# A hybrid mixer and MoE block on one core: whole-block transfers for all ten places of the weights' ring

## The chip, the cores and the metric

The kernel runs on one core of a Trainium2 chip. The metric is the device time of one execution in microseconds (us); lower is better. Three runs of the kernel before give a median of 1217.1 us (1215.6 to 1217.73).

## The reference, cut to what matters

One transformer block over 256 tokens of width 1024, all in float32:

```python
mod = jax.nn.silu(c) @ w_ada[l] + b_ada[l]                  # six rows: sh1, sc1, ga1, sh2, sc2, ga2
h = rms_norm(x, norm_w[l, 0]) * (1 + sc1) + sh1
y = hybrid_mixer(h, w_in[l], conv_w[l], a_log[l], dt_bias[l], a_norm_w[l], rel_bias[l], w_out[l])
x = x + ga1 * rms_norm(y, norm_w[l, 1])
h = rms_norm(x, norm_w[l, 2]) * (1 + sc2) + sh2
y = moe_ffn(h, w_router[l], b_router[l], w_up[l], b_up[l], w_down[l], b_down[l])
x = x + ga2 * rms_norm(y, norm_w[l, 3])
```

`hybrid_mixer` is a gated delta rule (4 heads of 128, chunks of 64 tokens) beside an attention over a band of chunks with a relative bias (8 heads of 64). `moe_ffn` routes each token to 4 of 32 experts:

```python
hu = xe @ w_up[e] + b_up[e]
glu = jnp.minimum(hu[:, :D_EXPERT], 7.0)
lin = jnp.clip(hu[:, D_EXPERT:], -7.0, 7.0)
act = glu * jax.nn.sigmoid(1.702 * glu) * (lin + 1)
out = act @ w_down[e] + b_down[e]
```

`w_up[e]` is 1024 x 2048 and `w_down[e]` 1024 x 1024, so one expert has 12.6 MB of weights and the 32 experts 402.7 MB; each is read once.

## The kernel before, in words

The mixer comes first, then the router, then the experts. The weights of the mixer are packed on the host into blocks of 2 MB, 128 partitions by 4096 floats (`wpre`); `wload` (L79) brings one block into one buffer in one transfer, `hload` (L84) in two halves. The weights of each expert are packed likewise as six blocks of 2 MB (`wexp`), here called chunks: chunks 0 to 3 are the four quarters of `w_up`, chunks 4 and 5 the halves of `w_down`.

**Groups.** The experts are worked off in 14 groups, written as `ORDER = "PQPPSQPPSQPPPP"`: P is a pair of experts with 64 token places each, Q four experts with 32, S a single one with 128. `group` (L1119) runs chunks 0 to 5 in order. For a chunk, `eload` (L1101) issues the loads of that chunk for every expert of the group, and `expert_mm` (L1112) multiplies: its outer loop runs over the eight slices k of the contraction and its inner loop over the experts, so that with P the two experts' matmuls alternate (L1117). Behind the chunks 0 and 1, and 2 and 3, comes the activation (`act`, on DVE and ACT) and four transposes of its result (L1145); chunks 4 and 5 read the transposed result, the first four slices from chunks 0 and 1, the last four from chunks 2 and 3. The result of a down chunk is copied (L1163) and spread to the tokens by four matmuls (L1166).

**The ring.** The loads go round a ring of ten places of 2 MB, `RINGTAGS` (L23): wB, w0, wC, wE, w1, wD, wF, wh, wA, wx. Both w0 and w1 are printed as `w_f` in the trace. Eight places are fixed blocks of 16 KB in each partition. The other two are each put together from two pool tiles of 8 KB: "wh" from two tiles of tag wh, "wx" from one tile of tag wh and one of tag h2. `wslot` (L1092) hands them out. A place of two tiles needs two transfers, and `eload` then splits every load of the same chunk in two:

```python
m = 8 // max(pieces, max(len(ts) for ts in tss))
```

The transfers are issued first halves first, one for each expert, then second halves. `PIECES = {0: 2, 1: 2, 2: 2}` (L34) asks for halves for chunk 5 of group 0 and for all chunks of groups 1 and 2; the last chunk of the last group goes in four pieces of 512 KB.

**Order.** All these loads are issued by SP, one queue in program order. From group 1 on the experts' numbers come from the routing (`sig`, cast by DVE at L1218), and SP reads each of them with a load of its own (L1276) before the group's first transfer. A scheduler orders the instructions of each engine when the kernel is built; the source gives it the order of emission, pools and dependencies.

**The mixer's buffers.** The pool tag wh (3 tiles) also holds the high halves that `split` (L205) makes of the mixer's float32 blocks; tag h2 holds in turn `xt`, `whx`, `strip` (the relative bias, loaded at L748, masked by POOL at L750, added to the scores by DVE at L767) and `yb`. `delta_out` (L882) transposes the delta rule's output, 128 tokens at a time (L893), and splits it into two halves (ACT L896, DVE L897); the output projection's matmuls (L231) read those.

**Down biases.** `b_down` is loaded in group 1 in two pieces of 64 KB (`bdn`), each just ahead of the two matmuls that use it (L1294).

Of the kernel before, what the change touches and what calls it, by code (L numbers as in the profile page):

```python
# [8 lines left out]
F32 = mybir.dt.float32  # L9
F32R = mybir.dt.float32r  # L10
# [10 lines left out]
D = 1024  # L21
NE = 32
RINGTAGS = ["wB", "w0", "wC", "wE", "w1", "wD", "wF", "wh", "wA", "wx"]  # L23
PB = {"mm": 3, "dl": 3, "tp": 2}
# [8 lines left out]
ZPOS = [0, 2, 0, 0]  # L33
PIECES = {0: 2, 1: 2, 2: 2}  # L34


SINGLES, QUADS = 2, 3
ORDER = "PQPPSQPPSQPPPP"
WH = 3
RS_N = -2.0 * (-2.0 * (-2.0) ** 3) ** 3  # L40
# [9 lines left out]
def block_kernel(ctx, tc, x, small, rows, rel_ext, wpre, wexp, b_up, b_down, out,  # L50
                 dbg=None, stop=None):
    nc = tc.nc
    P = 128
# [6 lines left out]


    base = (nc.sbuf_base + 31) // 32 * 32
    ctx.enter_context(nc.sbuf_tensor("fixed", [P, 8 * 4096], F32))
    fixed = {}
    for i, tag in enumerate(("w0", "w1", "wA", "wB", "wC", "wD", "wE", "wF")):
        fixed[tag] = [nc.alloc_sbuf_tensor_at(f"{tag}_{d_}", (P, 4096), dt, offset=base + 16384 * i).ap()
                      for d_, dt in (("f", F32), ("r", F32R))]
# [25 lines left out]
    def k2(name, shape=(P, 512), dt=F32):  # L93
        return mem.tile(list(shape), dt, tag="k2", bufs=K2, name=name)
# [76 lines left out]

    xt = mem.tile([P, 2, D], F32, tag="h2", name="xt")
    csil = const.tile([P, 8], F32, name="csil")
# [29 lines left out]
    nsp = [0]  # L203

    def split(w, kv=None, steps=1, extra=None, copy=None):  # L205


        sr, wl = w
        kv = kv or KV
        wh = extra  # L210
        if wh is None:
            wh = mem.tile([P, 2048], F32, tag="wh", bufs=WH, name="wh").bitcast(F32R)
        kn = sr.shape[1]
        wh = wh.rearrange("p (k n) -> p k n", k=kn)
# [125 lines left out]
    kqT = mem.tile([P, 4, 2, 256], F32, tag="acc", name="kqT")  # L340
    whx = mem.tile([P, 2048], F32R, tag="h2", name="whx")
    spr = bank("dl")
# [403 lines left out]
    def attention(blS):  # L746
        strip = mem.tile([P, 8, 256], F32, tag="h2", name="strip")
        nc.sync.dma_start(strip, bass.AP(tensor=rel_ext.tensor, offset=rel_ext.offset,  # L748
# [114 lines left out]
    pos = steps(mixed(), 17)  # L863
    yb = mem.tile([P, 2, D], F32, tag="h2", name="yb")
    wo.append(hload(19, "w1", 4))
# [226 lines left out]
    def wslot(tag):  # L1092

        if tag in ("wh", "wx"):
            ts = [mem.tile([P, 2048], F32, tag="wh", bufs=WH, name="wh") if tag == "wh" or i == 0 else
                  mem.tile([P, 2048], F32, tag="h2", name="wx") for i in range(2)]
        else:
            ts = [block(tag)]
        return [t.rearrange("p (k n) -> p k n", n=512) for t in ts]
# [19 lines left out]
    def group(load, xg, wt, sels, first=False, mid=None, done=None):  # L1119
# [155 lines left out]
    for gi, grp in enumerate(groups):  # L1275
# [7 lines left out]
        if gi + 1 < len(groups):  # L1283
            ohog = prep(groups[gi + 1])
        cur = group(lambda j: eload(regs, j, 4 if (gi, j) == (len(groups) - 1, 5) else PIECES.get(gi, 1) if gi or j == 5 else 1), cur[0], cur[1], sels, gi == 0, mid, done if gi == len(groups) - 1 else None)
        if gi == 1:
            overflow()

            for n in range(2):
                bdn = k2("bdn", (NE, 512))  # L1290
                nc.sync.dma_start(bdn, b_down[:, n * 512:(n + 1) * 512])
                for a in range(2):
                    b_ = bank("tp")
                    T.matmul(b_, tqs[:, 256 + a * 128:256 + (a + 1) * 128], bdn, start=True, stop=True)  # L1294
                    V.tensor_add(acc[:, a, n * 512:(n + 1) * 512], acc[:, a, n * 512:(n + 1) * 512], b_)
# [100 lines left out]
```

## Time and profile before

| | before |
|---|---|
| median of 3 runs | 1217.1 us (1215.6 to 1217.73) |
| the profiled execution | 1217.74 us, of which the span of the trace is 1215.9 us |
| PE busy | 1052.1 us (87%) |
| DVE, ACT, POOL busy | 371.0, 192.8, 93.8 us (31%, 16%, 8%) |
| mean granted clock of TensorE | 0.942 |
| moved by DMA | 451.95 MB, 372 GB/s over the span |

In the trace's rows PE is the matrix engine (PEld its weight loads), DVE, ACT and POOL the vector, scalar and general engines, SP the engine that issues the loads, and SPq its queue. A row of the timeline has start, duration (both us), engine, line, operation, output<-inputs, count, and in brackets the idle time just before and who ended it. A matmul of `expert_mm` appears as two rows. A row of the DMA view has the transfers of one kind: count, KB of one, and the median time in us from issue to landing. A window's row is explained at its first use.

### The profile page before, as it was taken

The numbers are of one execution on the slowest core, as the hardware profiler recorded it, in microseconds if no ns is written. First come the engines' busy times: TensorE is split into PE (matmuls) and PEld (weight loads), VectorE is DVE, ScalarE is ACT, GpSimd is POOL, SyncE is SP. The second block draws the span as 40 slices with busy tenths as digits, with TensorE's granted clock in tenths as the row PEclk, the third lists the DMA queues.
The fourth block names the chain that finished last, engine by engine and source line by source line (L and its number), as shares of the span: only waits on it lengthen the run. The fifth ranks groups of instructions, "written<-read, shape, count | busy, mean of one in ns | idle before, by whom it ended". The sixth has DMA issues, their size and how long they took to land. (4 is left out here: it accounts for less than half of the span.)

```text
span 1215.9 us, 14799 instructions
## 1 busy us (share of the span) xinstructions
PE 1052.1 (87%) x5891; PEld 502.7 (41%) x5891; DVE 371.0 (31%) x852; ACT 192.8 (16%) x392; POOL 93.8 (8%) x61
## 2 busy tenths in 40 slices
PE   4878999999987799999996779989976798898995
PEld 2667997683431133334431133434421142333331
DVE  5587888564202112121211002122211011111113
ACT  3544315331101001010100001010100001010101
POOL 1435424010000000000000000000000000000001
PEclk9989999979998899999997899999997799999998
DMA  9923455696999999999999999999999999999993
GB/s 362 390 76 139 143 208 241 263 424 221 420 421 420 421 416 410 430 422 424 428 415 426 424 423 429 424 427 425 419 427 424 423 427 422 427 424 423 428 419 130
DMA packets 51464, 451.95 MB, mean 372 GB/s; under 512 B 5760, under 2 KB 7424, under 8 KB 9408
## 3 DMA queue, kind: packets, MB, share of 16 engines
q1 hardware_dynamic: 51392, 450.97, 89.6%
q8 instruction: 48, 0.79, 0.3%
q14 instruction: 24, 0.20, 0.0%
HBM read 449.50 MB, written 1.05 MB: 371 GB/s over the span
## 5 line engine op out<-in xcount | busy, mean ns | idle before, releaser
L1117 PE MATMUL dl<-w_f,xg 128*64 128x512 f32 (+1 forms) x224 | 114.8, 659 | 10.9 <-DMA w_f<-in_wexp_dram 10.9
L1171 DVE TENSOR_TENSOR acc<-acc,mm 128x512 f32<-128x512 f32 x52 | 35.8, 688 | 240.8 <-PE mm L1166 240.8
L1117 PE MATMUL mm<-w_f,xg 128*64 128x512 f32 (+2 forms) x208 | 94.4, 603 | 4.8 <-DMA w_f<-in_wexp_dram 4.8
L1273 POOL TENSOR_TENSOR wF_f<-acc,m_row 128x512 f32<-128x512 f32 x3 | 3.8, 1275 | 948.0 <-DVE acc L1171 948.0
L1117 PE MATMUL dl<-wh,xg 128*64 128x512 f32 (+2 forms) x144 | 70.2, 631 | 3.9 <-DMA wh<-in_wexp_dram 3.9
L1117 PE MATMUL dl<-wD_f,xg 128*64 128x512 f32 (+1 forms) x128 | 65.3, 661 | 3.3 <-DMA wD_f<-in_wexp_dram 3.3
L1117 PE MATMUL dl<-wE_f,xg 128*64 128x512 f32 (+2 forms) x112 | 56.7, 660 | 9.5 <-DMA wE_f<-in_wexp_dram 9.5
L1166 PE MATMUL mm<-yg,wts 128*128 128x512 f32 x112 | 54.5, 614 | 11.7 <-ACT yg L1163 10.7
L1135 ACT ACTIVATE sg<-gm 128x512 f32<-128x512 f32 x28 | 17.7, 631 | 289.1 <-DVE gm L1133 265.2
L1117 PE MATMUL mm<-wB_f,xg 128*64 128x512 f32 (+2 forms) x128 | 59.3, 610 | 0.0
L1117 PE MATMUL dl<-wC_f,xg 128*64 128x512 f32 (+2 forms) x112 | 56.7, 652 | 2.5 <-DMA wC_f<-in_wexp_dram 2.5
L1117 PE MATMUL dl<-wF_f,xg 128*64 128x512 f32 (+2 forms) x112 | 54.8, 628 | 3.0 <-DMA wF_f<-in_wexp_dram 3.0
L1117 PE MATMUL mm<-wh,xg 128*64 128x512 f32 (+1 forms) x144 | 56.8, 594 | 0.0
L998 PEld LDWEIGHTS tp<-oh,x 128*128 128x128 f32 x432 | 50.8, 193 | 12.2 <-issue 10.4
L998 PE MATMUL tp<-oh,x 128*128 128x128 f32 x432 | 54.7, 280 | 0.7 <-ACT aT__3401 L1146 0.7
L1117 PE MATMUL mm<-wE_f,xg 128*64 128x512 f32 (+1 forms) x112 | 49.6, 594 | 2.9 <-DMA wE_f<-in_wexp_dram 2.9
L1117 PE MATMUL dl<-wB_f,xg 128*32 128x512 f32 (+1 forms) x96 | 49.0, 647 | 3.5 <-DMA wB_f<-in_wexp_dram 3.5
L1008 DVE TENSOR_SCALAR xg<-tp,mc,mc 128x128 f32<-128x128 f32 x52 | 19.6, 406 | 104.0 <-PE dl L1117 95.3
L1163 ACT COPY yg<-dl 128x512 f32<-128x512 f32 x27 | 15.8, 586 | 223.7 <-PE dl L1117 223.7
L1117 PE MATMUL mm<-wC_f,xg 128*64 128x512 f32 (+1 forms) x112 | 50.0, 594 | 0.0
L1133 DVE TENSOR_SCALAR gm<-dl 128x512 f32<-128x512 f32 x14 | 9.7, 692 | 128.7 <-PE dl L1128 128.7
L1117 PEld LDWEIGHTS dl<-w_f,xg 128*64 128x64 f32 (+1 forms) x224 | 28.2, 135 | 45.6 <-issue 25.5
(634 smaller groups left out, 2244.8 us busy)
## 6 DMA issues: line engine op xcount, KB each, us to landing
wh<-in_wexp_dram SPq DMA_DIRECT2D x57, 1024.0 KB, 24.6
w_f<-in_wexp_dram SPq DMA_DIRECT2D x26, 2048.0 KB, 25.8
wA_f<-in_wexp_dram SPq DMA_DIRECT2D x36, 1024.0 KB, 22.2
wF_f<-in_wexp_dram SPq DMA_DIRECT2D x36, 1024.0 KB, 29.5
wE_f<-in_wexp_dram SPq DMA_DIRECT2D x15, 2048.0 KB, 29.4
wC_f<-in_wexp_dram SPq DMA_DIRECT2D x15, 2048.0 KB, 27.0
wB_f<-in_wexp_dram SPq DMA_DIRECT2D x13, 2048.0 KB, 22.1
wD_f<-in_wexp_dram SPq DMA_DIRECT2D x13, 2048.0 KB, 34.2
```

The lines of the kernel that those rows point to most:

```text
L998: T.matmul(b_[:, k * 128:(k + 1) * 128], x2[:, a, half(n)][:, k * 128:(k + 1) * 128], oh[:, a], start=a == tiles[0], stop=a == tiles[-1])
L1008: V.tensor_scalar(xg[:, k], src, mc, sc, op0=ALU.mult, op1=ALU.add)
L1117: T.matmul(b_[i * n:(i + 1) * n, :], lhs[:, k, i * n:(i + 1) * n], w(k), start=k == 0, stop=last and k == 7)
L1133: V.tensor_scalar(gm, bs[0], 7.0, None, op0=ALU.min)
L1135: S.activation(sg, gm, AF.Sigmoid, scale=1.702)
L1163: S.copy(yg, b_)
L1166: T.matmul(cb, wt[:, a], yg, start=True, stop=True)
L1171: V.tensor_add(acc[:, a, sl], acc[:, a, sl], cb)
L1273: (V if a and n else G).tensor_mul(fin[:, 0, a, sl], acc[:, a, sl], m3_row[:, sl])
```

## The change

Two more fixed blocks, wG and wH, take the places of "wh" and "wx", so that all ten places are alike. `wslot` is gone; `eload` issues one transfer of 2 MB for each place, two for chunk 5 of group 0, and four for the last chunk of the last group. The lower half of wH and the two halves of wG hold the high halves that `split` makes, in turn; the upper half of wH (`h2`) holds what tag h2 held. In the first group the matmuls of chunks 0 and 1 are emitted under a manual schedule of PE. `b_down` is loaded as one tile ahead of the groups. The later lines shift by up to 5 up or down: L1109 becomes L1104, L1117 becomes L1112, L1276 becomes L1280, L893 becomes L898.

```diff
-RINGTAGS = ["wB", "w0", "wC", "wE", "w1", "wD", "wF", "wh", "wA", "wx"]
+RINGTAGS = ["wB", "w0", "wC", "wE", "w1", "wD", "wF", "wG", "wA", "wH"]
...
-PIECES = {0: 2, 1: 2, 2: 2}
...
-    ctx.enter_context(nc.sbuf_tensor("fixed", [P, 8 * 4096], F32))
+    ctx.enter_context(nc.sbuf_tensor("fixed", [P, 10 * 4096], F32))
...
+    highs = [fixed["wH"][1][:, 0:2048], fixed["wG"][1][:, 0:2048], fixed["wG"][1][:, 2048:4096]]
+
+    def h2(dt=0):
+        return fixed["wH"][dt][:, 2048:4096]
...
-    xt = mem.tile([P, 2, D], F32, tag="h2", name="xt")
+    xt = h2().rearrange("p (a n) -> p a n", a=2)
...
-            wh = mem.tile([P, 2048], F32, tag="wh", bufs=WH, name="wh").bitcast(F32R)
+            wh = highs[nsp[0] % 3]
+            nsp[0] += 1
...
-        strip = mem.tile([P, 8, 256], F32, tag="h2", name="strip")
+        strip = h2().rearrange("p (h k) -> p h k", h=8)
...
-        tss = [wslot(slot()) for _ in regs]
-        m = 8 // max(pieces, max(len(ts) for ts in tss))
+        ts = [block(slot()).rearrange("p (k n) -> p k n", n=512) for _ in regs]
+        m = 8 // pieces
...
-        b0 = up(0, load(0))
-        g0 = act([b0, up(1, load(1))])
+        if first:
+
+            with tc.manual_schedule(engines={mybir.EngineType.PE}):
+                b0 = up(0, load(0))
+                b0b = up(1, load(1))
+            g0 = act([b0, b0b])
+        else:
+            b0 = up(0, load(0))
+            g0 = act([b0, up(1, load(1))])
...
+    bdn = mem.tile([NE, D], F32, tag="ga2", name="bdn")
+    nc.sync.dma_start(bdn, b_down)
...
-        cur = group(lambda j: eload(regs, j, 4 if (gi, j) == (len(groups) - 1, 5) else PIECES.get(gi, 1) if gi or j == 5 else 1), cur[0], cur[1], sels, gi == 0, mid, done if gi == len(groups) - 1 else None)
+        cur = group(lambda j: eload(regs, j, 4 if (gi, j) == (len(groups) - 1, 5) else 2 if (gi, j) == (0, 5) else 1), cur[0], cur[1], sels, gi == 0, mid, done if gi == len(groups) - 1 else None)
```

The change also moves instructions. On PE, the rows of the first group's chunks 0 and 1 read the same before and after, names and lines apart: under the manual schedule some matmuls of chunks 2 and 3 (on wF and wh, now wG) still stand among those of chunk 0. At the end of the mixer the eight transposes of `delta_out`, of which four stood ahead of the output projection and four among its matmuls (L893), now stand together ahead of it (L898). Three more places follow.

SP, in the mixer, the issues of the loads around the strip's; before:

```order
L81 DMA wF_f<-in_wpre_dram 128x4096
L748 DMA strip<-in_rel_ext_dram 128x8x256
L81 DMA wF_f<-in_wpre_dram 128x4096
L87 DMA w_f<-in_wpre_dram 128x2048 x2
L1109 DMA wA_f<-in_wexp_dram 128x2048 x2
L81 DMA wB_f<-in_wpre_dram 128x4096
```

and after (wH_f is `strip` in its new place):

```order
L85 DMA wF_f<-in_wpre_dram 128x4096 x2
L753 DMA wH_f<-in_rel_ext_dram 128x8x256
L85 DMA wB_f<-in_wpre_dram 128x4096
L91 DMA w_f<-in_wpre_dram 128x2048 x2
L1104 DMA wA_f<-in_wexp_dram 128x4096
L1188 DMA bdn<-in_b_down_dram 32x1024
```

The strip now stands behind both wF blocks, the wB block ahead of the w blocks, and the load of the down biases behind the first expert load.

SP, where the ring's second round begins (TENSOR_LOAD is the reading of one expert's number); before, with 4 readings between the first w_f and wC and 10 between wE and the last w_f (w1):

```order
L1109 DMA wB_f<-in_wexp_dram 128x2048
L1109 DMA w_f<-in_wexp_dram 128x2048
L1276 TENSOR_LOAD sig
...
L1109 DMA wC_f<-in_wexp_dram 128x2048
L1109 ISA
L1109 DMA wE_f<-in_wexp_dram 128x2048
...
L1109 DMA w_f<-in_wexp_dram 128x2048
```

and after:

```order
L1104 DMA wB_f<-in_wexp_dram 128x2048
L1104 DMA w_f<-in_wexp_dram 128x2048
L1280 TENSOR_LOAD sig
...
L1104 DMA wC_f<-in_wexp_dram 128x4096
L1104 ISA
L1104 DMA wE_f<-in_wexp_dram 128x4096
...
L1104 DMA w_f<-in_wexp_dram 128x4096
```

Now 9 readings stand ahead of wC, 11 between wE and w_f (w1), and each of the transfers is a whole place.

PE, in the last group, from the end of chunk 3 (dl<-wF, wh) into chunk 4 (dl<-wA with its partner); before:

```order
L1128 MATMUL dl<-bup,sel 64x512
L1117 MATMUL dl<-wA_f,aT__6164 64x512
L1117 MATMUL dl<-wh,aT__6164 64x512
...
L1145 MATMUL tp<-ident,gm 128x128 x4
L1117 MATMUL dl<-wA_f,aT__6164 64x512
L1117 MATMUL dl<-wx,aT__6164 64x512
```

and after:

```order
L1123 MATMUL dl<-bup,sel 64x512
L1112 MATMUL dl<-wA_f,aT__5980 64x512
L1140 MATMUL tp<-ident,gm 128x128 x4
L1112 MATMUL dl<-wH_f,aT__5980 64x512
L1112 MATMUL dl<-wA_f,aT__5980 64x512
```

Before, four slices of chunk 4 stand ahead of the transposes and read the places' first halves (wA, wh). Now one matmul on wA stands ahead of them, and all the others behind them and behind the first on wH.

## Rows read from the trace of the kernel before

**Rows 1.** Windows, whole span; columns from:to, length, busy of PE, PEld, DVE, ACT, POOL, PEclk, DMA share, GB/s

```profile
300.00:600.00 300.00, 270.56 (x1260) 103.78 (x1257) 61.01 (x149) 27.75 (x54) 0.00 (x0) 0.95 1.01 419
...
900.00:1190.00 290.00, 246.88 (x1156) 85.67 (x1158) 41.63 (x72) 23.59 (x46) 0.00 (x0) 0.93 1.01 423
1143.60:1168.10 24.50, 21.50 (x95) 7.04 (x92) 4.14 (x6) 1.42 (x3) 0.00 (x0) 1.00 1.01 426
```

**Rows 2.** Waits of SP's queue: who was waited for, us in total, times, longest

```profile
SPq L1109 <- DMA w_f<-in_wexp_dram: 133.9, 43, 5.8
```

**Rows 3.** Timeline of SP, expert loads: issues while transfers of 1 MB land

```profile
343.18 0.33 SPq L1109 DMA_DIRECT2D wE_f<-in_wexp_dram  x1
...
400.26 0.33 SPq L1109 DMA_DIRECT2D w_f<-in_wexp_dram  x1
```

**Rows 4.** Timeline of SP: issues while transfers of 2 MB land

```profile
1148.58 0.33 SPq L1109 DMA_DIRECT2D wh<-in_wexp_dram  x1
...
1168.17 0.33 SPq L1109 DMA_DIRECT2D wx<-in_wexp_dram  x1
```

**Rows 5.** DMA view, issues from 295 to 1195 us: transfers of 1 MB, first and last

```profile
wh<-in_wexp_dram SPq DMA_DIRECT2D x54, 1024.0 KB, 24.6
...
wE_f<-in_wexp_dram SPq DMA_DIRECT2D x8, 1024.0 KB, 18.0
```

**Rows 6.** Timeline of SP where the ring's second round begins

```profile
294.85 0.37 SPq L1109 DMA_DIRECT2D wC_f<-in_wexp_dram  x1
...
301.71 0.34 SPq L1109 DMA_DIRECT2D w_f<-in_wexp_dram  x1
...
308.46 0.33 SPq L1109 DMA_DIRECT2D wh<-in_wexp_dram  x1
...
325.64 0.33 SPq L1109 DMA_DIRECT2D wA_f<-in_wexp_dram  x1
```

**Rows 7.** DMA view: the issues at 308.46, 215.96 (into an empty queue) and 178.14

```profile
wh<-in_wexp_dram SPq DMA_DIRECT2D x1, 1024.0 KB, 18.2
...
wF_f<-in_wpre_dram SPq DMA_DIRECT2D x1, 2048.0 KB, 7.4
...
wF_f<-in_wpre_dram SPq DMA_DIRECT2D x1, 2048.0 KB, 8.6
```

**Rows 8.** Windows in the mixer's second half

```profile
190.00:205.00 15.00, 12.57 (x120) 10.06 (x117) 14.80 (x28) 11.03 (x28) 8.68 (x7) 1.00 0.84 334
...
240.00:257.00 17.00, 14.64 (x60) 11.22 (x60) 11.24 (x34) 5.90 (x11) 5.92 (x4) 0.90 1.00 428
```

**Rows 9.** Timeline of PE at the output projection

```profile
242.59 3.00 PE L231 MATMUL dl<-whx,wC_r 128*128 128x512 f32 x7 [1.74 <-DVE wC_r L897]
```

**Rows 10.** Timeline of SP, POOL and DVE around the strip

```profile
178.14 0.33 SPq L81 DMA_DIRECT2D wF_f<-in_wpre_dram  x1
...
173.09 1.51 POOL L750 TENSOR_SCALAR strip<-strip 64x512 f32<-64x512 f32 x1 [15.56 <-DMA strip<-in_rel_ext_dram]
...
184.11 1.29 DVE L767 TENSOR_TENSOR w_f<-mm,strip 128x512 f32<-128x512 f32 x2 [0.30 <-PE mm L762]
```

**Rows 11.** DMA view: the issues at 1148.58 (chunk 3) and 1168.17 (chunk 4)

```profile
wh<-in_wexp_dram SPq DMA_DIRECT2D x1, 1024.0 KB, 29.4
...
wx<-in_wexp_dram SPq DMA_DIRECT2D x1, 1024.0 KB, 19.8
```

**Rows 12.** Timeline of PE, last group: chunk 2 begins, chunk 3, chunk 5 begins

```profile
1168.09 1.12 PE L1117 MATMUL dl<-wD_f,xg 128*64 128x512 f32 x1 [0.28 <-DMA wD_f<-in_wexp_dram]
...
1176.89 0.59 PE L1117 MATMUL dl<-wh,xg 128*64 128x512 f32 x1
...
1183.76 0.38 PE L1128 MATMUL dl<-bup,sel 96*64 96x512 bf16 x1
...
1192.32 0.59 PE L1117 MATMUL dl<-wB_f,aT__6164 128*64 128x512 f32 x1
```

**Rows 13.** Timeline of DVE, last group: the second activation

```profile
1184.90 0.69 DVE L1139 SCALAR_TENSOR_TENSOR gm<-lc,gm 128x512 f32<-128x512 f32 x1
```

More of the change, by code (lines that the diff above doesn't have):

```diff
@@ L33 @@
 ZPOS = [0, 2, 0, 0]
-PIECES = {0: 2, 1: 2, 2: 2}
 SINGLES, QUADS = 2, 3
 ORDER = "PQPPSQPPSQPPPP"
-WH = 3
 RS_N = -2.0 * (-2.0 * (-2.0) ** 3) ** 3
@@ L62, in block_kernel @@
     base = (nc.sbuf_base + 31) // 32 * 32
-    ctx.enter_context(nc.sbuf_tensor("fixed", [P, 8 * 4096], F32))
+    ctx.enter_context(nc.sbuf_tensor("fixed", [P, 10 * 4096], F32))
     fixed = {}
-    for i, tag in enumerate(("w0", "w1", "wA", "wB", "wC", "wD", "wE", "wF")):
+    for i, tag in enumerate(("w0", "w1", "wA", "wB", "wC", "wD", "wE", "wF", "wG", "wH")):
         fixed[tag] = [nc.alloc_sbuf_tensor_at(f"{tag}_{d_}", (P, 4096), dt, offset=base + 16384 * i).ap()
@@ L340, in block_kernel @@
     kqT = mem.tile([P, 4, 2, 256], F32, tag="acc", name="kqT")
-    whx = mem.tile([P, 2048], F32R, tag="h2", name="whx")
+    whx = h2(1)
     spr = bank("dl")
@@ L863, in block_kernel @@
     pos = steps(mixed(), 17)
-    yb = mem.tile([P, 2, D], F32, tag="h2", name="yb")
+    yb = h2().rearrange("p (a n) -> p a n", a=2)
     wo.append(hload(19, "w1", 4))
@@ L1090, in slot @@
         return RINGTAGS[(rtag[0] - 1) % len(RINGTAGS)]
[L1092 to L1099, printed above, removed]
     def eload(regs, j, pieces=1):
-        tss = [wslot(slot()) for _ in regs]
-        m = 8 // max(pieces, max(len(ts) for ts in tss))
+        ts = [block(slot()).rearrange("p (k n) -> p k n", n=512) for _ in regs]
+        m = 8 // pieces
         for k in range(0, 8, m):
-            for reg, ts in zip(regs, tss):
+            for reg, t in zip(regs, ts):
                 src = wexp[reg * 6 + j] if isinstance(reg, int) else wexp[bass.ds(reg * 6 + j, 1)].rearrange("o p n -> p (o n)")
-                kt = 8 // len(ts)
-                nc.sync.dma_start(ts[k // kt][:, k % kt:k % kt + m].rearrange("p k n -> p (k n)"), src[:, k * 512:(k + m) * 512])
-        return [lambda k, ts=ts: ts[k * len(ts) // 8][:, k % (8 // len(ts)), :] for ts in tss]
+                nc.sync.dma_start(t[:, k:k + m].rearrange("p k n -> p (k n)"), src[:, k * 512:(k + m) * 512])
+        return [lambda k, t=t: t[:, k, :] for t in ts]
     def expert_mm(b_, lhs, ws, last=True):
@@ L1289, in block_kernel @@
             for n in range(2):
-                bdn = k2("bdn", (NE, 512))
-                nc.sync.dma_start(bdn, b_down[:, n * 512:(n + 1) * 512])
                 for a in range(2):
                     b_ = bank("tp")
-                    T.matmul(b_, tqs[:, 256 + a * 128:256 + (a + 1) * 128], bdn, start=True, stop=True)
+                    T.matmul(b_, tqs[:, 256 + a * 128:256 + (a + 1) * 128], bdn[:, n * 512:(n + 1) * 512], start=True, stop=True)
                     V.tensor_add(acc[:, a, n * 512:(n + 1) * 512], acc[:, a, n * 512:(n + 1) * 512], b_)
```

## The prediction, made before the changed kernel had run

> **What bounds the kernel now.** I read the windows first. From 300 us to 1190 us the DMA share is 1.01 and the rate 419 to 426 GB/s, while PE is busy 85 to 90% of each window [rows 1]. So in the experts' stage, three quarters of the time, the DMA engines are what is full, and PE waits for weights. The waits of SP's queue say the same: SP issues a load when an earlier one has landed (133.9 us in 43 waits for one tile's loads alone) [rows 2]. An issue in this stage therefore stands for a landing, and the spacing of issues on SP's timeline is the price of a transfer. A faster mixer or router counts in full, because it starts this stream earlier; a faster PE inside the stream counts nothing; behind the last landing PE and the closing chain count in full again. The change touches each of these three parts.
>
> The sum is made against the profiled execution, 1217.74 us (span 1215.9 us and 1.8 us around it), which stands 0.6 us above the median of 1217.1 us.
>
> **Term 1, the size of the transfers: -6.5 us.** While transfers of 1 MB land, 23 issues lie between 343.18 and 400.26 [rows 3]: 57.08 / 23 = 2.482 us each, 4.963 us for one place of 2 MB. While transfers of 2 MB land, 4 intervals lie between 1148.58 and 1168.17 [rows 4]: 19.59 / 4 = 4.898 us. (What lands there was issued earlier; the eighth transfer before the one just issued.) A place in one transfer is thus 0.065 us cheaper, some 1.3%. The DMA view has nine kinds of transfers of 1 MB between 295 and 1195 us, of which the first is x54 and the last x8 [rows 5]; they add up to 200, so 100 places. The change turns all of them into one transfer each: 100 x 0.065 = 6.5 us off the stream. Bounds: 100 places are 209.7 MB. By the windows, at 419 GB/s against 423 the gain is 500.5 - 495.7 = 4.8 us, at 419 against 426 it is 8.2 us [rows 1]; these windows mix both sizes and other work, so I take the spacings. The coarser places also come free later, but the ring holds 20 MB and SP waits for landings here, so I cost this at nothing; the cover is what is still on its way when PE frees a place, and without it the DMA engines would stand still.
>
> **Term 2, the ring's second round: -1.8 us.** Before, wC's half is issued at 294.85, and the tenth half from there, wh, at 308.46 [rows 6]; it lands 18.2 us later [rows 7], at 326.6. By then 10 MB have come in since wC's issue, with holes: the two halves of wC and wE last 5.0 us, and the next issue, held up by 10 readings of experts' numbers, comes only at 301.71, 6.9 us after wC's [rows 6]. After the change 9 readings instead of 4 stand ahead of wC. Less wE's own issue, those 10 took about 0.6 us each, so wC goes out 5 x 0.6 = 3.0 us later, at 297.85. A block of 2 MB into an empty queue lands after 7.4 us [rows 7], so wC lands at 305.25, and four more places behind it, without a hole (two places are 9.8 us of transfers, 11 readings 6.6 us), at 305.25 + 4 x 4.9 = 324.85. That is the same 10 MB 1.8 us sooner. Bounds: 0, if another hole eats it, to -4.8, if the queue is still full at 297.85 and wC's later issue costs nothing. Loading the down biases early takes two small transfers out of group 1 and puts one into the mixer; I put it at 0, hidden by the idle DMA of the mixer.
>
> **Term 3, the end of the mixer: -1.0 us.** Two things move against each other. For the change: both `delta_out` transposes now precede the output projection, so the split of the second half can run beside its first matmuls. PE idles 1.74 us there for DVE's split [rows 9]; all that PE idles in the two windows of this half with gaps is 2.43 us (190 to 205) and 2.36 us (240 to 257) [rows 8], so the gain can't exceed 4.8 us. Against it: the strip's load is queued behind the wF block that SP issues at 178.14 [rows 10] and that lands 8.6 us later [rows 7], at 186.7. The strip's 1 MB comes 2.5 us behind it, at 189.2, and POOL's pass of 1.51 us makes it 190.7, where DVE read it at 184.11 before [rows 10]: 6.6 us late. Queued behind it on SP are the wB block and the loads of the output projection's weights; on DVE, the attention's chain. PE has the delta rule's chain placed ahead of the attention now, which covers most of this. Bounds: -4.8 to +6.6 us. I take -1.0, nearest to the wait that the order of PE plainly removes (1.74 us), less a little for the strip.
>
> **Term 4, the tail: +2.5 us.** In the last group, chunks 3 and 4 came as halves, first halves first. The last half of chunk 3 was issued at 1148.58 [rows 4] and landed 29.4 us later [rows 11], at 1178.0, but PE had begun on this wh at 1176.89 [rows 12], on first halves. Chunk 4 is complete at 1168.17 + 19.8 = 1187.97 [rows 4, 11]; PE had done half of it by then and began chunk 5 at 1192.32 [rows 12]. Now, in the same frame (the last landing unmoved), wG is usable only when all of it is in, at 1178.1 (two places of 4.9 us before 1187.9). Chunk 3 takes from 1176.89 to the end of its bias matmul, 1183.76 + 0.38 = 1184.14 [rows 12], 7.25 us, and so ends at 1185.35. DVE's activation, which ended 1.45 us behind it before (1184.90 + 0.69) [rows 13], ends at 1186.8, the transposes fit in by 1187.6, and wH lands at 1187.97. Only then can the alternating matmuls of chunk 4 go on. Sixteen pairs at 0.43 us, the spacing inside chunk 3 (7.25 us less its biases over 16), take 6.9 us, so chunk 5 begins at 1194.85 instead of 1192.32. What follows (chunk 5, its spreading, the closing chain) is longer than what is left to land, so the 2.5 us reach the end. Bounds: +1.2, if only the later start of chunk 3 comes through, to +4.2: PE would idle some 2 us ahead of chunk 3 and again ahead of chunk 4, and when chunk 2 began behind a gap its matmuls took 1.12 us instead of 0.59 us [rows 12], the lower clock of 1.2 GHz; four pairs of matmuls at twice their 0.43 us would be 1.7 us more.
>
> A rule of the Trainium skill bears on this term (page Perfetto Trace Analysis, section DMA Optimizations): splitting transfers lets some work start sooner, and it pays where the DMA engines are generally idle. By that condition a split should bring nothing here, where they are busy, and the tail would cost 0 and the sum be 1207.8; the rows of chunks 3 and 4 show PE starting on first halves in a full stream, and I go by the rows.
>
> The manual schedule costs and gains nothing, since the matmuls of chunks 0 and 1 stand in the same order as before.
>
> **Sum.** 1217.74 - 6.5 - 1.8 - 1.0 + 2.5 = 1210.9 us; 0.6 less for the median, **1210.3 us**. A difference under 0.2% (2.4 us, that is 1214.7 to 1219.5) can't be told from no change.
>
> **Rivals.**
> - *The mixer's end gains all it can.* PE's idle time in [rows 8] goes: -4.8 instead of -1.0, **1206.5 us**. For it: the wait of [rows 9] is removed by order alone. Against: the late strip.
> - *The ring stalls, or the tail runs at the lower clock.* wA can be issued as a whole only when chunk 4 of group 0 is done, at 325.64, when its second half went before [rows 6]; by term 2 the places ahead of it land until 329.8, and an issue needs 7.4 - 4.9 = 2.5 us until its data flow, so the margin is 1.6 us. If it is missed by 2 us, 1212.3; with the lower clock's 1.7 us, **1214.0 us**.
> - *The size does not pay.* If the 1.3% between [rows 3] and [rows 4] comes from where they lie in the program (gathers and activations run beside the halves) and not from size, term 1 is 0: **1216.8 us**, no change. For it: the stream's long windows differ by 1% as well, 419 and 423 GB/s [rows 1]. Against: both spacings hold over many intervals.
> - *Slower.* The strip's 6.6 us pass through whole: attention's chain on DVE, and PE behind it, wait for POOL's pass at 190.7, the output projection and the router begin later by it, and so does the second round. PE, idle for that long, then runs at the lower clock for a while, the same 1.7 us: 1217.74 - 6.5 - 1.8 + 6.6 + 1.7 + 2.5 = 1220.2, **1219.6 us** for the median, and more if anything on SP behind the strip slips too. It decides from a mixer 8.3 us late. Against: PE had no gap of this size in the mixer, and now has more independent work to cover one.
> - *The change doesn't do what it says.* For the manual schedule this is so and priced at 0. For the loads it can't be: the order of SP has whole places throughout.
>
> **How the numbers follow.** Forecast 0.48; mixer's full gain 0.15; ring or clock 0.18; size does not pay 0.12; slower 0.07. The forecast's own bounds, one term at its end at a time, make it 1207.3 to 1212.1. The range reaches from 1205.5, just below the second case, to 1214.5, just above the third, and leaves out the last two. Faster by over 0.2%: 0.48 + 0.15 + 0.16 = 0.79. Within 0.2%: the rest of the third case and nearly all of the fourth, 0.14. Slower: 0.07.
>
> **What would show it.** After the change SP's expert loads should be spaced 4.9 us from 340 us to the last group, and every window of the stream stand at 423 GB/s or more; spacings of 4.96 us would refute term 1. wC should be issued near 297.9, less whatever the mixer gains, with one hole ahead of it and none behind; a hole behind 325 us would be the ring's stall. The first expert matmul should start 1 us sooner (4.8 sooner to 6.6 later are the bounds), and `delta_out`'s splits end no wait over 1 us. In the last group PE should wait for wG and wH, and the time from the last landing to the end grow by 2.5 us. The prediction is wrong if the mixer slips by more than 3 us, if that growth exceeds 4 us, or if the stream's rate doesn't rise.

## The result, and the profile after

The changed kernel takes 1231.99 us (median of 4 runs, 1230.37 to 1236.29), the kernel before beside it 1217.41 us (4 runs). The ratio is 1.0125 [1.0101, 1.0148]: **1.25% slower, 14.6 us**, where 0.6% faster was forecast. The profiled execution took 1230.37 us, its span is 1228.5 us.

Four marks cut each trace by the terms of the prediction: the first expert matmul (end of mixer and router), the moment at which 35.7 MB of expert weights have landed (the tenth half from wC in [rows 6], or the fifth whole place), the last landing, and the end. Times in us; the last column is the median against the kernel before on the same chip. Names beginning with e are the experiments below. A single profiled trace stands within some 3 us of its kernel's median, and two traces of the same mixer code can differ by as much: e5 and e7 begin the experts at 278.10 and 274.64 us.

| kernel | mixer and router | second round | stream | tail | span | median, ratio |
|---|---|---|---|---|---|---|
| before | 275.39 | 51.23 | 871.25 | 18.01 | 1215.9 | |
| after | 295.14 | 50.67 | 862.31 | 20.40 | 1228.5 | 1231.99, 1.0125 [1.0101, 1.0148] |
| e1, order of the high halves | 284.58 | 50.69 | 862.03 | 22.06 | 1219.4 | 1221.60, 1.0033 [1.0016, 1.0050] |
| e2, e1 and one ada block later | 286.99 | 50.45 | 862.08 | 21.78 | 1221.3 | 1223.33, 1.0031 [0.9998, 1.0064] |
| e3, no manual schedule, late biases | 297.23 | 49.07 | 865.04 | 20.50 | 1231.8 | 1232.88, 1.0125 [1.0079, 1.0170] |
| e4, halves again | 295.95 | 51.36 | 868.36 | 17.12 | 1232.8 | 1232.48, 1.0117 [1.0070, 1.0165] |
| e5, places from a pool | 278.10 | 50.02 | 863.25 | 20.54 | 1211.9 | 1211.82, 0.9969 [0.9958, 0.9980] |
| e6, e5 and halves at the end | 277.58 | 48.88 | 863.98 | 17.14 | 1207.6 | 1209.14, 0.9944 [0.9928, 0.9960] |
| e7, e5 with late biases | 274.64 | 49.46 | 864.44 | 20.50 | 1209.0 | 1213.83, 0.9983 [0.9969, 0.9996] |
| e8, after and halves at the end | 292.77 | 50.47 | 862.29 | 17.19 | 1222.7 | 1226.52, 1.0092 [1.0073, 1.0111] |
| e9, e2 and a second ada block later | 287.09 | 50.74 | 861.89 | 20.45 | 1220.2 | 1223.24, 1.0066 [1.0049, 1.0083] |
| e10, one ada block later alone | 294.74 | 50.32 | 861.75 | 21.75 | 1228.6 | 1228.55, 1.0093 [1.0064, 1.0122] |

Before to after, the columns change by +19.75, -0.56, -8.94 and +2.39 us, in sum +12.6. The prediction had -1.0, -1.8, -6.5 and +2.5: three terms are near, and **the mixer is wrong by 21 us**.

The stream first. Windows of after (columns as in [rows 1]):

```profile
360.00:600.00 240.00, 209.87 (x1001) 81.74 (x996) 47.44 (x111) 20.18 (x39) 0.00 (x0) 0.94 1.01 428
600.00:900.00 300.00, 262.99 (x1290) 103.60 (x1288) 53.67 (x118) 26.69 (x52) 0.00 (x0) 0.95 1.01 428
900.00:1190.00 290.00, 244.87 (x1181) 90.79 (x1182) 42.56 (x76) 23.55 (x46) 0.00 (x0) 0.95 1.01 428
```

It runs at 428 GB/s in all three, where [rows 1] had 419 to 426, at the same DMA share. Before: the DMA engines were as full, and moved less.

Now the mixer, at two places. DVE of after, from 141 us (start, duration, then the row as in the timeline of [rows 10]):

```profile
141.75 0.49 DVE L729 TENSOR_SCALAR wF_f<-wF_f,csil 128x512 f32<-128x512 f32 x1 [4.90 <-DMA wF_f<-in_wpre_dram]
142.28 1.54 DVE L731 SCALAR_TENSOR_TENSOR wF_f<-wF_f,csil 128x512 f32<-128x512 f32 x2
143.73 0.69 DVE L224 TENSOR_TENSOR w_r<-w_f,wH_r 128x512 fp32r<-128x512 f32 x1
144.33 4.57 DVE L731 SCALAR_TENSOR_TENSOR wF_f<-wF_f,csil 128x512 f32<-128x512 f32 x2
148.93 1.40 DVE L646 TENSOR_TENSOR wE_f<-wE_f,dl 64x512 f32<-64x512 f32 x2
```

The same two steps of DVE before (L641 became L646, L724 became L729); this swap is not among the moves that the section on the change lists:

```profile
142.40 1.40 DVE L641 TENSOR_TENSOR wE_f<-wE_f,dl 64x512 f32<-64x512 f32 x2 [0.38 <-PE dl L601]
143.83 2.02 DVE L724 TENSOR_SCALAR wF_f<-wF_f,csil 128x512 f32<-128x512 f32 x1
```

L646 is a subtraction of the delta rule's solver, on which PE waits. L729 and L731 work off a block of `w_ada` for the modulation rows, which the solver doesn't read. Before, the subtraction stood ahead; after, the `w_ada` job does, and DVE, working in order, sits 4.90 us for the job's load with the subtraction behind it. PE of after shows what that did, here and 48 us later:

```profile
149.66 1.64 PE L606 MATMUL dl<-wE_f 64*64 64x64 f32 x13 [6.48 <-DVE wE_f L646]
...
151.38 2.47 PE L606 MATMUL dl<-wE_f,Lm 64*64 64x64 f32 x29
...
197.25 4.15 PE L672 MATMUL dl<-wB_f,wE_f 64*64 64x128 f32 x32 [2.50 <-DVE wE_f L646]
```

The gap of 6.48 us is **slip 1**. Until 144 us PE was 2 us ahead of the kernel before, behind it 8 us late. The 29 matmuls at 151.38 took 2.47 us here and 1.25 us before, as PE's row of before shows; the granted clock from 150 to 155 us is 0.50 here and was 1.00 before:

```profile
146.51 1.25 PE L601 MATMUL dl<-wE_f,Lm 64*64 64x64 f32 x29
```

**Slip 2** begins with the strip. SP, POOL and DVE of after:

```profile
161.25 25.49 SPq L85 DMA_DIRECT2D wF_f<-in_wpre_dram  x2
188.59 0.39 SPq L753 DMA_DIRECT2D wH_f<-in_rel_ext_dram  x1
```

```profile
198.91 1.49 POOL L755 TENSOR_SCALAR wH_f<-wH_f 64x512 f32<-64x512 f32 x1 [5.99 <-DMA wH_f<-in_rel_ext_dram]
```

```profile
196.12 0.49 DVE L729 TENSOR_SCALAR wF_f<-wF_f,csil 128x512 f32<-128x512 f32 x1 [4.00 <-DMA wF_f<-in_wpre_dram]
196.52 1.39 DVE L646 TENSOR_TENSOR wE_f<-wE_f,dl 64x512 f32<-64x512 f32 x2
```

The strip goes out 21.6 us later than before, where SP had

```profile
166.97 0.39 SPq L748 DMA_DIRECT2D strip<-in_rel_ext_dram  x1
```

It now goes out behind the second wF block at 186.41, and its pass on POOL comes 25.8 us later than in [rows 10]. The row of SP's waits names another reason than that place in the queue: the strip is now the upper half of block wH, whose lower half is a high half, and its load waits for the readers of that half, the matmuls of L236 (1.8 us in total, once, 1.8 the longest):

```profile
SPq L753 <- PE mm L236: 1.8, 1, 1.8
```

So the attention can't begin, PE has less to do beside the delta rule, and when DVE sits for a `w_ada` load again (4.00 us) PE runs dry for 2.50 us. What follows costs more than the gap. Windows of after, PE alone (length, PE busy, granted clock, DMA share, GB/s):

```profile
195.00:200.00 5.00, 2.75 (x22) 0.75 0.29 94
200.00:205.00 5.00, 5.00 (x49) 0.84 0.03 7
205.00:210.00 5.00, 5.00 (x21) 0.50 0.83 292
210.00:215.00 5.00, 5.00 (x25) 0.55 0.30 128
215.00:220.00 5.00, 5.00 (x40) 1.00 0.60 195
...
225.00:230.00 5.00, 4.43 (x23) 0.82 0.61 252
230.00:235.00 5.00, 5.00 (x24) 0.50 0.00 0
```

PE has no gap from 200 to 220 us, yet from 205 to 215 us works at or near 1.2 GHz (0.50); before, the granted clock was 1.00 in every window from 180 to 240 us, as in this one:

```profile
205.00:210.00 5.00, 4.83 (x37) 1.00 0.63 265
```

By an estimate (each window's busy time by what its clock lacks of 1.00), the windows of after lose 9.5 us of PE's work to the clock, against 2.50 us in the gap.

The shared block shows once more, in the output projection. There `yb` lives in the upper half of wH, and a high half of the weights in the lower one. PE of after:

```profile
267.52 2.09 PE L236 MATMUL dl<-wH_r,wC_r 128*128 128x512 f32 x8 [2.63 <-POOL wH_f L918]
...
274.91 2.09 PE L236 MATMUL mm<-wH_r,wC_r 128*128 128x512 f32 x8 [1.59 <-DVE wH_f L921]
```

L918 and L921 write `yb`, which these matmuls do not read, and by the rows the matmuls wait for them, 4.2 us in all.

The tail came as forecast. PE of after, last group, beginnings of chunk 3, of the transposes and of chunk 4's second place:

```profile
1188.21 0.64 PE L1112 MATMUL dl<-wG_f,xg 128*64 128x512 f32 x1 [2.48 <-DMA wG_f<-in_wexp_dram]
...
1197.02 0.66 PE L1140 MATMUL tp<-ident,gm 128*128 128x128 f32 x4 [1.50 <-DVE gm L1134]
1198.03 0.64 PE L1112 MATMUL dl<-wH_f,aT__5980 128*64 128x512 f32 x1 [0.36 <-DMA wH_f<-in_wexp_dram]
```

PE waits for the whole of wG and again, briefly, for wH, where [rows 12] show it starting on halves without a wait; the first matmuls behind the gaps took 0.64 us, so the clock hardly fell here. In e1, e2 and e10, which have the same last group, it did fall, and their tails are 21.75 to 22.06 us. A window of e1 (columns as in the windows of PE alone above):

```profile
1185.00:1190.00 5.00, 3.47 (x14) 0.79 1.00 399
```

### The profile page after: what moved, and what is told of

The parts are those of the page before. It is cut to its first block, busy times and chain, and to the rows that moved or that the text cites. A ratio compares the mean times of both kernels' runs of the same rounds, so it can differ in the third digit from the quotient of the medians.

```text
span 1228.5 us, 14430 instructions
## 1 busy us (share of the span) xinstructions
PE 1051.3 (86%) x5891; PEld 519.3 (42%) x5891; DVE 373.5 (30%) x852; ACT 192.7 (16%) x392; POOL 94.2 (8%) x61
## 5 line engine op out<-in xcount | busy, mean ns | idle before, releaser
L1112 PE MATMUL dl<-w_f,xg 128*64 128x512 f32 (+1 forms) x224 | 113.6, 659 | 13.7 <-DMA w_f<-in_wexp_dram 13.7
L1112 PE MATMUL mm<-w_f,xg 128*64 128x512 f32 (+2 forms) x208 | 92.7, 594 | 0.9 <-DMA w_f<-in_wexp_dram 0.9
L1112 PE MATMUL dl<-wD_f,xg 128*64 128x512 f32 (+1 forms) x128 | 62.6, 644 | 6.7 <-DMA wD_f<-in_wexp_dram 6.7
L1112 PE MATMUL dl<-wG_f,xg 128*64 128x512 f32 (+2 forms) x112 | 52.9, 621 | 7.6 <-DMA wG_f<-in_wexp_dram 7.6
L1112 PE MATMUL mm<-wB_f,xg 128*64 128x512 f32 (+2 forms) x128 | 57.4, 595 | 0.0
L1112 PE MATMUL dl<-wF_f,xg 128*64 128x512 f32 (+2 forms) x112 | 54.0, 628 | 3.8 <-DMA wF_f<-in_wexp_dram 3.8
L1112 PE MATMUL dl<-wE_f,xg 128*64 128x512 f32 (+2 forms) x112 | 54.4, 640 | 2.0 <-DMA wE_f<-in_wexp_dram 2.0
L1112 PE MATMUL dl<-wB_f,xg 128*32 128x512 f32 (+1 forms) x96 | 51.3, 686 | 4.3 <-DMA wB_f<-in_wexp_dram 4.3
L1112 PE MATMUL dl<-wC_f,xg 128*64 128x512 f32 (+2 forms) x112 | 54.7, 640 | 0.0
L1112 PE MATMUL mm<-wE_f,xg 128*64 128x512 f32 (+1 forms) x112 | 49.6, 594 | 0.0
L1112 PE MATMUL mm<-wC_f,xg 128*64 128x512 f32 (+1 forms) x112 | 49.5, 593 | 0.0
L1112 PEld LDWEIGHTS dl<-w_f,xg 128*64 128x64 f32 (+1 forms) x224 | 28.7, 134 | 44.7 <-issue 25.8
L1112 PE MATMUL mm<-wH_f,xg 128*64 128x512 f32 (+1 forms) x96 | 42.4, 595 | 1.0 <-DMA wH_f<-in_wexp_dram 1.0
```

Source lines behind the costliest of these rows:

```text
L1112: T.matmul(b_[i * n:(i + 1) * n, :], lhs[:, k, i * n:(i + 1) * n], w(k), start=k == 0, stop=last and k == 7)
```

## The experiments

**e1. The order of the high halves.** Slip 2 says that the strip is late because the lower half of its block is in use. So the three high halves are given out in another order:

```diff
-    highs = [fixed["wH"][1][:, 0:2048], fixed["wG"][1][:, 0:2048], fixed["wG"][1][:, 2048:4096]]
+    highs = [fixed["wG"][1][:, 0:2048], fixed["wH"][1][:, 0:2048], fixed["wG"][1][:, 2048:4096]]
```

> Edit: only the order in which the three high-half places take turns (wG lower, wH lower, wG upper instead of wH lower, wG lower, wG upper). Theory A (strip and a high half share the block wH, and the strip's load waits for the last high half's readers and so falls behind a wF block on SP): the strip's load goes out some 14 us earlier, PE's order of the attention returns, and the later of the two slips of the mixer (+11.6 of +19.75 us) goes: 1220 us (1217 to 1223), first expert matmul near 283.5. Rivals B (manual schedule or early down biases) and C (whole transfers in the mixer): no change, 1230 to 1234 us.

Measured: 1221.60 us (10 runs), 1.0033 [1.0016, 1.0050]; the first expert matmul at 284.58 us. SP and PE of e1:

```profile
175.53 0.39 SPq L753 DMA_DIRECT2D wH_f<-in_rel_ext_dram  x1
186.85 0.33 SPq L85 DMA_DIRECT2D wF_f<-in_wpre_dram  x1
```

```profile
149.99 1.65 PE L606 MATMUL dl<-wE_f 64*64 64x64 f32 x13 [6.21 <-DVE wE_f L646]
```

The strip goes out 13 us earlier, ahead of the second wF block; PE's granted clock is 1.00 in all windows from 180 to 240 us, and PE has no wait for L918 or L921. Slip 1 is still there, and it is all that is left: setting each matmul beside the same one before, PE is 1.9 us early at 141 us, 7.7 late at 148, 7.9 late at 233 and 9.2 late at 283. In after it is 8.2 us late at 176 and 19.75 at 283; that difference is slip 2. One line of buffer order, with no arithmetic or transfer changed, is worth 10.4 us in the medians.

**e2. One `w_ada` block later as well.** `ADAPOS` says at which step of the mixer a `w_ada` block's job is emitted.

```diff
-ADAPOS = [5, 31, 6, 12, 8, 31, 19, 32]
+ADAPOS = [5, 31, 6, 12, 10, 31, 19, 32]
```

> Edit: that of e1, and the third of the wF jobs (a block of w_ada worked off by DVE) is emitted two steps later (position 10 instead of 8), so that on DVE it stands behind the solver's subtraction (L646) that PE waits for. Theory A2 (the first slip, +8 to +9.6 us near 145 us, is this one swap on DVE, with the lower clock that follows): both slips go, first expert matmul at 273 to 277, 1211 us (1207 to 1215). If the swap isn't the cause: as e1, near 1220.

Measured: 1223.33 us: a miss by the median. Four of the 10 runs lie from 1213.57 to 1217.91, below every run of e1 (1220.49 and up), and six from 1223.05 to 1227.58; the profiled one is of the upper group, and why there are two is open. So what follows holds for the upper group; in the lower one taking slip 1 away as well did pay. Slip 1 is gone (no gap over 1 us from 120 to 199 us), but the next block's job has moved ahead of L674. PE of e2, and two windows:

```profile
199.90 4.09 PE L678 MATMUL dl<-wE_f,wB_f 64*128 64x64 f32 x29 [3.43 <-DVE wE_f L674]
```

```profile
205.00:210.00 5.00, 5.00 (x21) 0.50 1.02 436
210.00:215.00 5.00, 5.00 (x23) 0.50 0.59 251
```

In this execution the wait was removed at one place and came back at another, with the lower clock behind it.

**e9. The second block later too.** e2 with `ADAPOS` entry 6 at 22 instead of 19, which puts the new offender between the two L674.

> e2 with one more table entry: the w_ada block whose job on DVE (L729 and its L731s) stood ahead of L674 in e2 is given a later place (22 instead of 19), and now stands between the two L674. Theory (two slips of the mixer, both of them work on DVE or a load on SP standing ahead of a step of the delta rule, and nothing else): with e1's order of the high halves and both jobs behind the steps that they held up, the mixer is about as long as in e5, chunk 0 begins near 279 us (275 to 282), the granted clock from 200 to 220 us is over 0.9, and the time is 1213 to 1216 us. Rival (the mixer with fixed blocks shared by halves is longer in itself, whatever the order on DVE): chunk 0 stays near 287 us as in e2, and the time at 1221 to 1225 us.

Measured: 1223.24 us, 1.0066 [1.0049, 1.0083]; first expert matmul at 287.09. The wait for L674 went and a third one came. DVE and PE of e9:

```profile
210.96 1.23 DVE L224 TENSOR_TENSOR w_r<-w_f,wH_r 128x1024 fp32r<-128x1024 f32 x1 [1.55 <-ACT wH_r L222]
212.22 0.69 DVE L695 TENSOR_TENSOR vn<-wE_f,dl 64x512 f32<-64x512 f32 x1
```

```profile
212.97 1.43 PE L701 MATMUL dl<-vn,kdt 64*128 64x128 f32 x5 [4.48 <-DVE vn L695]
```

Now a split of an output projection's weight block (L224), waiting for ACT, stands ahead of the delta rule's L695. The rival's number came out; whether its reason did is open, since the mixer has a wait of the same kind at yet another place.

**e10. One `w_ada` block later alone**, in the changed kernel, the high halves as there. With after, e1 and e2 it makes a square.

> The changed kernel with e2's table entry alone (the third w_ada block at place 10 instead of 8), the high halves in the changed kernel's order. It completes the square of e1 and e2. If the two slips add: slip 1 (8 to 9.6 us) goes and the strip's wait stays, chunk 0 begins near 286 us (284 to 289) and the time is 1222 to 1225 us. Rival (the strip's load would have come late by its own wait however early the mixer was, so that slip 1 was covered by slip 2): chunk 0 stays at 292 us or later, and the time is 1228 us or more. Third way, as in e2 (the next w_ada job gets ahead of a step of the delta rule in place of the first): a wait of PE of over 2 us for DVE's L674 or L646 between 190 and 205 us, and some 3 us less of the gain.

Measured: 1228.55 us (1223.11 to 1230.32), 1.0093 [1.0064, 1.0122]; first expert matmul at 294.74. Slip 1 is gone: PE, 2.9 us behind after's until 142 us, is 4 to 7 us ahead of it from 158 to 198 us. From 247 us on the two are level again (0.5 us). PE of e10, and its windows:

```profile
200.74 4.37 PE L678 MATMUL dl<-wE_f,wB_f 64*128 64x64 f32 x29 [3.77 <-DVE wE_f L674]
```

```profile
205.00:210.00 5.00, 5.00 (x25) 0.50 1.01 431
...
225.00:230.00 5.00, 5.00 (x27) 0.50 0.00 0
230.00:235.00 5.00, 5.00 (x29) 0.87 0.00 0
```

Behind a gap of 3.77 us the five windows from 205 to 230 us are all at 0.50, with PE busy throughout; by the same estimate as for after, 15 us of PE's work. The waits for L918 and L921 are there as in after. As the traces stand, removing slip 1 brought 0.4 us of the mixer, removing slip 2 10.6, both 8.2. But e10's trace is of the slowest of its four runs (1230.32; the fastest took 1223.11), and it is 2.4 us behind after's at 60 us already, where the granted clock was 0.89 instead of 0.94; by the medians e10 is 3.4 us faster than after. So the third way of the expectation is what happened, and it ate most of the gain of 8 to 9.6 us, not some 3 us of it. Whether the two slips add is open: with the lower four runs of e2 they would.

**e3. Manual schedule undone, biases late again.**

```diff
-        if first:
-
-            with tc.manual_schedule(engines={mybir.EngineType.PE}):
-                b0 = up(0, load(0))
-                b0b = up(1, load(1))
-            g0 = act([b0, b0b])
-        else:
-            b0 = up(0, load(0))
-            g0 = act([b0, up(1, load(1))])
+        b0 = up(0, load(0))
+        g0 = act([b0, up(1, load(1))])
...
+                bdn = k2("bdn", (NE, 512))
+                nc.sync.dma_start(bdn, b_down[:, n * 512:(n + 1) * 512])
```

> Edit: the manual schedule of the first two chunks undone, and the down biases loaded late as before. Theory A: neither matters, 1232 us (1229 to 1235), mixer late as after the change. Rival B: the mixer returns, near 1212 us.

Measured: 1232.88 us, 1.0125 [1.0079, 1.0170], as after: neither part made the kernel slow. The stream is 2.7 us longer, the second round 1.6 us shorter, 1.1 us in sum.

**e4. Halves again, on the fixed blocks.** The loads as before, everything else as after.

```diff
-        m = 8 // pieces
+        m = 8 // max(pieces, 2 if any((rtag[0] - 1 - q) % 10 in (7, 9) for q in range(len(regs))) else 1)
...
-        cur = group(lambda j: eload(regs, j, 4 if (gi, j) == (len(groups) - 1, 5) else 2 if (gi, j) == (0, 5) else 1), cur[0], cur[1], sels, gi == 0, mid, done if gi == len(groups) - 1 else None)
+        cur = group(lambda j: eload(regs, j, 4 if (gi, j) == (len(groups) - 1, 5) else {0: 2, 1: 2, 2: 2}.get(gi, 1) if gi or j == 5 else 1), cur[0], cur[1], sels, gi == 0, mid, done if gi == len(groups) - 1 else None)
```

> Edit: the loads go in halves again wherever they did before (every chunk with the eighth or tenth place, groups 0 to 2 as before), the ten fixed places stay. Theory A: the mixer stays late (first expert matmul near 295), the stream loses what whole transfers gave (+8.9 us from the 10th MB of the second round to the last landing) and the tail gets its 2.35 us back: 1238.5 us (1236 to 1241). Rival C (whole transfers of the first round delay the mixer): the mixer returns, near 1219.

Measured: 1232.48 us, below the expected range: by the medians e4 and after can't be told apart. The mixer is as long as in after (295.95), so the size of the transfers has no part in that. The stream is 868.36 - 862.31 = 6.05 us longer and the tail 3.28 us shorter: the two terms of size, each by itself. The stream is the steadier measure: in the eight traces with whole places (e6's and e8's last chunks aside) and early biases it lies between 861.75 and 863.98 us.

**e5. Ten whole places without sharing.** The kernel before, with its pool tiles of the mixer (tags wh and h2) in a pool of their own that is closed when the mixer ends, and wG and wH taken from a new pool behind it. Whole transfers and early biases as in the change, no manual schedule.

```diff
+    pst = ExitStack()
+    whp = pst.enter_context(tc.tile_pool(name="whp", bufs=1))
...
-        strip = mem.tile([P, 8, 256], F32, tag="h2", name="strip")
+        strip = whp.tile([P, 8, 256], F32, tag="h2", name="strip")
...
+    pst.close()
+    rp = ctx.enter_context(tc.tile_pool(name="rp", bufs=1))
+    for tag in ("wG", "wH"):
+        fixed[tag] = [rp.tile([P, 4096], F32, tag=tag, name=tag)]
```

> Edit: the kernel before, with the mixer's buffers kept as pool tiles (their own pool, given back when the mixer ends) and the two 16 KB places of the ring taken from the memory that they leave; whole transfers and early down biases as after the change, no manual schedule. DVE and SP stand in the order of before through the mixer. Theory A (all of the loss is the mixer's order, brought by the fixed places): first expert matmul at 274 to 278, whole transfers -6.1 to -8.9 us, second round about -0.6, tail +2.4 to +4: 1211.5 us (1208.5 to 1214.5), 3 to 8 us under before. If something else in whole places costs time (the ring starving), it stays at 1217 or above.

Measured: 1211.82 us (8 runs), 0.9969 [0.9958, 0.9980]. SP of e5, and two windows (columns as in [rows 1]):

```profile
169.39 0.39 SPq L750 DMA_DIRECT2D strip<-in_rel_ext_dram  x1
180.56 0.33 SPq L83 DMA_DIRECT2D wF_f<-in_wpre_dram  x1
```

```profile
205.00:220.00 15.00, 13.39 (x100) 9.74 (x100) 7.28 (x18) 5.99 (x16) 7.36 (x4) 1.00 0.44 167
...
600.00:900.00 300.00, 261.43 (x1332) 99.87 (x1334) 53.88 (x116) 24.39 (x47) 0.00 (x0) 0.95 1.01 427
```

The strip stands ahead of the wF block again, the clock holds, the mixer is 2.7 us longer than before instead of 19.75, and the stream keeps its gain. Of the 2.7 us, 1.9 are there at 60 us already, with a granted clock of 0.89 up to there instead of 0.94, and e7, with the same mixer, begins the experts 0.75 us earlier than before; so no loss of the mixer is left beyond the scatter. PE's longest gap from 130 to 280 us is 1.44 us.

**e6 and e8. Chunks 3 and 4 of the last group in halves**, in e5 and in after: `2 if (gi, j) == (0, 5)` becomes `2 if (gi, j) in ((0, 5), (len(groups) - 1, 3), (len(groups) - 1, 4))`.

> Edit: e5, and the last group's chunks 3 and 4 go in halves again. Theory: the tail from the last landing to the end returns to about 18 us (17 to 18.5) and the time falls by 2.4 to 4 us under e5: 1208.5 us (1205.5 to 1212).

> Edit: the changed kernel with the last group's chunks 3 and 4 in halves. By term 4 the tail shrinks by 2.4 to 3.3 us and nothing else moves: 1229.2 us (1227.5 to 1231.5), tail 17 to 18 us. If the last landing sets the end alone, no change: 1232.

Measured: e6 1209.14 us (6 runs), 0.9944 [0.9928, 0.9960], 2.7 us under e5; its tail is 17.14 instead of 20.54 us. e8 1226.52 us, 5.5 us under after and 1 us below the expected range. That is more than the tail's 3.2 us (20.40 to 17.19); in the trace the rest lies in the mixer, 2.4 us earlier, where nothing was edited, so it is scatter between profiled executions or chips. PE of e8 as chunk 3 and chunk 4's second place begin:

```profile
1182.86 0.59 PE L1112 MATMUL dl<-wG_f,xg 128*64 128x512 f32 x1
...
1192.20 0.64 PE L1112 MATMUL dl<-wH_f,aT__5980 128*64 128x512 f32 x1
```

Neither row has a wait now. **e6 is faster than both kernels.**

**e7. e5 with late biases.**

> Edit: e5 with the down biases loaded late, in group 1, as before the change. If the early load is worth what e3 and the changed kernel differ by in the stream (2.7 us from the 10th MB of the second round to the last landing), the time is 2 to 3 us above e5, 1214; by my price of the prediction (nothing), within 1 us of e5.

Measured: 1213.83 us (12 runs, 1210.78 to 1217.98), 2.0 us over e5, but with wide scatter; its stream is 1.2 us longer than e5's and its second round 0.6 us shorter. Loading the biases early is thus worth some 1 us in the sum of the two columns (1.1 by e3, 0.6 by e7), not the 0 that I gave it; the medians say 2.0 us, and more can't be said.

## Why the prediction was wrong, step by step

- **Term 1, size: right.** -6.5 us predicted, 6.05 measured by e4 against after. The rival "the size does not pay" falls: whole places move 428 GB/s in all three windows of after, and e4's halves, at the same places of the program, 423 to 425. The other 2.9 us of the stream's 8.94 are of the size that e3 shows in this column (2.7 us), where the biases are late and the manual schedule is undone; of these the second round of e3 gets 1.6 us back.
- **Term 2, second round: mis-sized.** -1.8 predicted, -0.56 measured. wC's issue came as worked out, 22.3 us behind the first expert matmul (317.41 less 295.14; predicted 22.5). "Four more places behind it, without a hole" was right too. SP's issues of after, and the DMA view of the same two:

```profile
317.41 0.37 SPq L1104 DMA_DIRECT2D wC_f<-in_wexp_dram  x1
...
330.99 0.35 SPq L1104 DMA_DIRECT2D wF_f<-in_wexp_dram  x1
```

```profile
wC_f<-in_wexp_dram SPq DMA_DIRECT2D x1, 2048.0 KB, 8.8
...
wF_f<-in_wexp_dram SPq DMA_DIRECT2D x1, 2048.0 KB, 14.8
```

wC lands at 326.2 and the fourth place behind it, wF, at 345.8: 19.6 us, 4.9 each. What was mis-sized is wC's own landing, 8.8 us behind its issue and not the 7.4 of [rows 7]; why is open. From wC's issue to 35.7 MB took 28.4 us, not 27.0.
- **Term 3, the end of the mixer: this step failed**, by 21 us. It asked the right question, what is late when the strip slips, and answered it in three wrong ways. First, "at 189.2" for the strip's landing took the wF block at its old time, 178.14, and gave the strip's load no wait of its own. In fact the mixer was 8 us late by then (186.41) and the load was issued at 188.59, right behind the readers of the other half of its block; e1 shows what the order of the halves is worth, 10.4 us. Second, the step looked at the last third of the mixer only, while the order of DVE had changed at 142 us, with L729 ahead of L646: the step doesn't name this swap and doesn't ask who waits for L646. Third, "PE has the delta rule's chain placed ahead of the attention now, which covers most of this" was a guess; PE ran dry for 2.50 us. Its gain did come: the wait of 1.74 us in [rows 9] is gone from after, and 4.2 us of waits for L918 and L921 took its place. (In e1 the eight transposes stand apart again, and PE waits 1.72 us for that split.) The range left the step's own upper bound out as well: "one term at its end at a time, make it 1207.3 to 1212.1" skips the +6.6 us, which make 1217.9 us.
- **The rival "Slower" had the place and the sign, not the size.** It priced the lower clock at 1.7 us, from four pairs of matmuls at the end of the kernel. In the mixer the clock was low for long stretches behind several of the gaps. By the estimate above, in windows of 1 us from 195 us to the first expert matmul, the clock took 16.6 us of PE's work in after and 21.6 in e10, against 8.5 before; PE's idle time there rose from 5.4 us to 10.1 and 10.2. So the clock cost some 8 and 13 us more than before, the gaps not quite 5.
- **Term 4, the tail: right**, the closeness in part luck. +2.5 predicted, +2.39 measured, and by the two mechanisms named (waits for wG and for wH). In e1, e2 and e10, where the clock fell too, the tail grew by 3.7 to 4.1 us: there the rival "or the tail runs at the lower clock" came on top, by the same estimate with 1.6 to 1.7 us, the size that it was given. The Trainium skill (page Perfetto Trace Analysis, section DMA Optimizations) names generally idle DMA engines as the case in which splitting may let the whole task end sooner; that a split brings nothing where they are busy is what the prediction made of it. Here, with the engines at 1.01, e6 gained 2.7 us and the tails of e6 and e8 shrank by 3.4 and 3.2 us.
- **The manual schedule: right** at 0 in the sum. Without it (e3, e5, e6, e7) wC goes out 20.1 us behind the first expert matmul instead of 22.3 and the second round is 48.9 to 50.0 us instead of 50.3 to 50.7, but the stream is longer by as much: with early biases the two columns add up to 912.1 to 913.0 us with it and 912.9 and 913.3 without.
- **What is shown and what stays open.** e5 gives the change without the shared blocks: 1211.8 us, 0.31% under the kernel before on its chip, where the forecast was 0.6%: the same sign, and some two thirds of the 6.8 us. So the mixer's time was lost through the shared blocks and the order that came with them, slip 2 by the place of the high halves (e1), slip 1 by the order on DVE, whose removal took the gap of 6.48 us away (e2, e10). Why the new buffers changed that order on DVE wasn't tried. Nor does any trace show an order on shared blocks without such a wait: those of e2, e9 and e10 each lack the one aimed at and have another, and none comes under e1's 284.58 us. The four faster runs of e2, of which there is no trace, may be such a case.

## What to carry to other kernels

Two buffers put into the two halves of one block can become one dependency, and even where no wait grows, the scheduler orders by the new dependencies: before costing such an edit, compare the order of every in-order engine along the whole critical chain and ask, for each job that waits for a load, what stands behind it. Price a new gap on PE by what the clock does afterwards as well as by its length. And where whole transfers win in a full stream, the last chunks may still want halves, because there nothing is left to cover the wait for a whole one.

## What the runs showed of the hardware that I had not expected

- The granted clock stayed at 0.50 from 205 to 230 us in e10, behind a gap of 3.77 us, although PE was busy for 5.00 us of every 5.00; 29 matmuls of L678 took 4.37 us there, and 32 of them 2.27 us in e1 at 1.00. In e5 it was 1.00 from 140 to 240 us, with no gap over 1.33 us in that time. But a gap isn't always ahead: in e9 it was 0.88 from 185 to 190 us and 0.50 from 190 to 195 us, with PE busy throughout from 170 us on.
- Two L731 on DVE took 4.57 us at 144.33 in after, where a pair takes 1.54 (142.28, same operands). POOL was at work beside them for most of that time, as its row shows; what the two share isn't shown by any run:

```profile
144.50 3.86 POOL L226 TENSOR_TENSOR w_r<-w_f,wH_r 128x1536 fp32r<-128x1536 f32 x1 [5.41 <-DVE w_r L224]
```

- Whole places brought 428 GB/s at the same DMA share of 1.01 at which halves moved 419: the share tells that the engines are busy, not how much they carry.
